# Layer 3's up-projection past the skew as two-by-two blocks in seven products

## The chip, the core and the metric

The kernel runs on one core of a Trainium2 chip. A core has five engines with a queue of instructions each: TensorE (matmuls, PE in the profile, its weight loads PEld), VectorE (DVE), ScalarE (ACT), GpSimd (POOL) and SyncE (SP, which only issues DMAs here). They work out of one on-chip memory (SBUF) and leave matmul results in eight banks of another (PSUM). The metric is device time of one execution in microseconds; the median of the runs shown is 2803.71 us.

## What is computed

The reference is one step of a backbone of four layers on 640 tokens of 1024 features: 512 tokens of a sample and 128 of a prompt, which share all weights. Every layer has a token mixer and then a gated ConvFFN, each between two LayerNorms. The part that matters here is the ConvFFN:

```python
def _conv_ffn(h, w_up, conv_w, conv_b, w_down):
    a, b = jnp.split(h @ w_up, 2, axis=-1)          # h: tokens x 1024, w_up: 1024 x 5632
    ap = jnp.pad(a, ((0, 0), (1, 1), (0, 0)))
    a = ap[:, :-2] * conv_w[0] + ap[:, 1:-1] * conv_w[1] + ap[:, 2:] * conv_w[2] + conv_b
    return (jax.nn.gelu(a) * b) @ w_down            # 2816 -> 1024
```

All is float32. The convolution reads the neighbouring tokens of a, in the sample and in the prompt separately.

## The kernel before, in words

Activations lie feature-major: a ktile is 128 features on the partitions by 640 tokens. Exactness comes from splitting each float32 operand into two parts of a shorter format, hi and lo, that add up to it (`unit` for weights, L157, `split` for activations, L167): ScalarE casts hi (L163, L169), VectorE subtracts it from the original for lo (L164, L170). A product is three matmuls, hi hi, hi lo and lo hi (`mm3`, L175 to L177). The 640 tokens are worked on in two halves, A of 256 and B of 384 columns.

The ConvFFN of a layer has 22 ktiles of 128 hidden features. Ktile j needs two units of weights of w_up, 2j for a and 2j + 1 for b, each [128, 8, 128] (512 KB); the input h is eight ktiles `hs`, hi and lo. Half A of ktiles 0 to 5 runs early, while half B of h is still being made (`ffn_pre`, L529); `skew` (L568) adds their half B, ktile 5 first, 0 last. Ktiles 6 to 21 follow in `up` (L581): for each of the two units the eight-ktile product of half A, then of half B, so 4 x 8 x 3 = 96 matmuls, half with 256 and half with 384 columns. `ffn_a` (L497) copies a out of PSUM on ScalarE into a padded row buffer `ap`. `ffn_g` (L505) then does the convolution (one ScalarE pass and two VectorE passes per segment, L512 and L514), the gelu (L516), the products with b, which is still in PSUM (L518, L519), and the split of the result into an `act` tile (L169, L170).

The down-projection runs in three chunks of ktiles, (0, 7), (7, 14) and (14, 22) (`FFN_CHUNKS`, L40); each chunk's products over its ktiles are added into x for eight output ktiles by VectorE (`evac`, L436). A chunk's down-projection is written behind the first ktile of the next chunk. The last chunk goes through `project` (L440), whose half A's LayerNorm lies beside half B's matmuls. In layers 0 to 2 the FFN also carries the next layer's modulation on VectorE; layer 3 has none.

Tiles come from pools with a fixed number of slots: `actp` 16 (activations in two parts), `hlp` 6 (weights in two parts, 8 KB per partition), `rawp` 4 (weights as loaded), `tmpp` 5, and in PSUM `mmp` 4, `bcp` 3, `stp` 1 banks. The program is not run in the order in which it is written: a scheduler takes, for each engine, the ready instruction that stands earliest in the text, by its own model of times, gives out slots as they come free in that model, and puts in the waits. The order is fixed before the run; on the chip each engine's queue is first in, first out.

Of the kernel before, what the change touches and what calls it, by code (L numbers as in the profile page):

```python
# [33 lines left out]
# half 0 runs ahead of half 1, and 2 of 3 (in front of the pooling, which reads neighbours)  # L34
HALVES = ((0, 256), (256, 640), (0, 384), (384, 640))
HW = 384
# (start, stop, group) with group 0 = sample, 1 = prompt
SEGS = (((0, 256, 0),), ((256, 512, 0), (512, 640, 1)), ((0, 384, 0),), ((384, 512, 0), (512, 640, 1)))
# ktiles of the FFN between its down-projections
FFN_CHUNKS = ((0, 7), (7, 14), (14, 22))  # L40
SKEW = {None: 7, 2: 6, 3: 6, 1: 6, 0: 6}
# units of a projection's weights that half B finds from half A
KEEP = {None: 4, (0, 0): 3, (1, 1): 5, (3, 1): 5, (1, 0): 3, (3, 0): 5}
# layer 0's modulation, blocks of 512 features, in plain float32
MOD32 = (2, 0)
# SKEW ktiles of the FFN run half A ahead of half B, 2 SKEW units of weights: the last SPLIT of them in split parts
# (SPLIT_AHEAD units ahead of their use), of which half B finds the last KEPT; h is split SPLIT_H units from the end
# [29 lines left out]
# columns of the packed per-partition vectors  # L77
# [33 lines left out]
class Kern:  # L111
    def __init__(self, ctx, tc, a):
# [4 lines left out]
        self.actp = P("actp", 16)  # L117
        self.hlp = P("hlp", 6)
# [38 lines left out]
    def unit(self, src, shape, e=None):  # L157
        """A piece of weights, split exactly into two float32r parts."""
        nc = self.nc
        r = self.raw(shape)  # L160
        self.load(r, src)
        hl = self.hlp.tile([128, 2] + list(shape[1:]), F32R, tag="hl", name=self.nm("hl"))
        nc.scalar.copy(hl[:, 0], r)  # L163
        (e or nc.vector).tensor_sub(hl[:, 1], r, hl[:, 0])  # L164
        return hl

    def split(self, dst, src, e=None):  # L167
        """dst [:, 0] + [:, 1] = src exactly."""
# [13 lines left out]
    def table(self, f, x):  # L182
        """Has the tables of an activation function loaded ahead of its use, once x is there."""
        self.nc.scalar.activation(self.small("tab", [128, 1]), x.bitcast(F32), f)

    def consts(self):
# [24 lines left out]
        self.cbc = cp.tile([128, 2, D], F32, name="cbc")  # L211
        self.aps = [cp.tile([128, T + 3], F32, name=f"ap{i}") for i in range(2)]
        self.bgq, self.bgf = [], 0.0
        # modulation [part, chunk, ktile, group]
        self.mod = [cp.tile([128, 6, NK, 2], F32, name=f"mod{i}") for i in range(DEPTH)]

    def cond_rows(self):
        """silu(cond) along the free dimension, on every partition."""
        nc = self.nc
        for g in range(2):  # L220
# [8 lines left out]
    def mod_post(self, L, ft, n, ps, lo=None):  # L229
        """Feature tiles ft .. ft + n (of one chunk) of the modulation of layer L, from its sums [128, n, 2]."""  # L230
# [42 lines left out]
    def mod_dve(self, L, f0, f1):  # L273
        """Feature tiles f0 .. f1 as dot products on the vector engine. Yields after each product."""
# [15 lines left out]
    def bg(self, n):  # L290
        """n steps (on average) of the background work."""
# [18 lines left out]
    def sums_new(self, half):  # L310
        """Sums of z and z^2 over the ktiles, per partition, of a half."""
# [64 lines left out]
    def centre(self, MU, half, ahead):  # L376
        """The ktiles of x of a half less their mean, some ahead of their use."""
# [10 lines left out]
    def ln1(self, t, R, L, which, half, k, S=None):  # L388
        """x <- LN(z) g + b on a ktile of a half."""
# [10 lines left out]
    def ln2(self, t, R, L, ch, half, k, box):  # L400
        """h = LN(x)(1 + scale) + shift on a ktile of a half."""
# [158 lines left out]
    def ffn(self, L, box, side, after):  # L560
# [55 lines left out]
        if L == 0:  # L616
            self.bgq.append(self.mod_dve(0, 40, 48))
# [782 lines left out]
```

## Time and profile before

| what | value |
|---|---|
| median of three runs | 2803.71 us (2803.0 to 2804.68) |
| profiled execution, first to last instruction | 2805.7 us, 2.0 above the median of the runs |
| TensorE busy | 2749.6 us, 98% |
| VectorE busy | 1973.0 us, 70% |
| ScalarE busy | 1240.0 us, 44% |
| GpSimd busy | 407.5 us, 15% |
| the DMA queue of SP | 341.74 MB, 38.7% of 16 engines' time |
| mean granted clock of TensorE | 0.987 |

The profile is of one execution. Durations of TensorE overlap, since matmuls are pipelined: the distance from start to start is what one costs in a row. Durations of VectorE and ScalarE overlap a little too, for the same reason. Layer 3's skew lies at 2362 to 2410 us, its `up` ktiles and down-projections behind that to the end.

### The profile page before, as it was taken

What the parts mean: (1) busy time and instruction counts of PE and PEld (TensorE: products, weight loads), DVE (VectorE), ACT (ScalarE), POOL (GpSimd) and SP (SyncE); (2) the same over time, 40 slices, a digit from 0 to 9 for tenths busy, and PEclk for the clock granted to TensorE, in tenths of its full rate; (3) what the DMA queues carried; (4) which work ended last, traced back from release to release, by engine and by line L of the source; (5) the groups of instructions that cost most, each with busy time, mean ns of one, the idle gap of its engine ahead of it and who ended that gap; (6) DMA issues with size and microseconds to landing.
All of it is one profiled execution on the core that took longest, in us unless ns stands there. A gap on an engine that the chain in (4) does not pass through costs nothing.

```text
span 2805.7 us, 46039 instructions
## 1 busy us (share of the span) xinstructions
PE 2749.6 (98%) x17826; PEld 2636.0 (94%) x17826; DVE 1973.0 (70%) x4263; ACT 1240.0 (44%) x2286; POOL 407.5 (15%) x417
## 2 busy tenths in 40 slices
PE   7999999999999999999999999999999999999998
PEld 4799999999989999999978999999799999999998
DVE  6879977857697887777587878775756558534344
ACT  5656232336496752323367423234532248423233
POOL 1250000024303300000442000005100042000003
PEclk9999999999999999999989999999999999999999
DMA  7735644432402445455104554542422224322221
GB/s 241 259 109 163 198 154 149 156 121 80 134 22 83 136 153 158 149 157 153 56 35 150 151 165 151 158 136 80 161 65 91 68 62 152 97 82 68 83 75 54
DMA packets 99932, 344.70 MB, mean 123 GB/s; under 512 B 11392, under 2 KB 14080, under 8 KB 99584
## 3 DMA queue, kind: packets, MB, share of 16 engines
q1 hardware_dynamic: 99712, 341.74, 38.7%
q8 instruction: 141, 2.31, 0.3%
q14 instruction: 79, 0.65, 0.1%
HBM read 336.19 MB, written 2.88 MB: 121 GB/s over the span
## 4 chain that ended last, share of the span: by engine, by line
PE 88%; DVE 5%; issue 2%; ACT 2%; DMA 2%; POOL 1%; POOLq 0%; ACTq 0%; SPq 0%; DVEq 0%
PE mm L175 26%; PE mm L176 26%; PE mm L177 26%; PE mm L487 2%; PE st L352 1%; PE mm L1157 1%; DVE hl L164 1%; DVE tmp L339 1%; DMA raw<-in_wmod 1%; PE mm L1247 1%; PE bc L372 1%; DVE lnt L383 1%; DVE act L170 0%; PE mm L1072 0%; DMA raw<-in_wup 0%
## 5 line engine op out<-in xcount | busy, mean ns | idle before, releaser
L177 PE MATMUL mm<-act,hl 128*128 128x384 f32 (+2 forms) x4928 | 1528.5, 310 | 3.2 <-DVE hl L164 3.2
L175 PE MATMUL mm<-act,hl 128*128 128x384 f32 (+2 forms) x4928 | 1531.5, 311 | 0.0
L176 PE MATMUL mm<-act,hl 128*128 128x384 f32 (+2 forms) x4928 | 1528.6, 310 | 1.2 <-POOL act L418 1.2
L177 PEld LDWEIGHTS mm<-act,hl 128*128 128x128 f32 x4928 | 935.1, 190 | 5.0 <-DVE hl L164 4.4
L176 PEld LDWEIGHTS mm<-act,hl 128*128 128x128 f32 x4928 | 935.9, 190 | 3.7 <-POOL act L418 1.8
L175 PEld LDWEIGHTS mm<-act,hl 128*128 128x128 f32 x4928 | 935.2, 190 | 3.2 <-ACT hl L163 0.6
L163 ACT CAST hl<-raw 128x1024 fp32r<-128x1024 f32 (+1 forms) x433 | 444.1, 1030 | 625.9 <-PE mm L177 560.1
L164 DVE TENSOR_TENSOR hl<-raw,hl 128x1024 fp32r<-128x1024 f32 (+1 forms) x428 | 526.0, 1231 | 67.4 <-ACT hl L163 65.1
L283 DVE SCALAR_TENSOR_TENSOR bc<-raw,cbc 128x512 f32<-128x512 f32 x608 | 406.2, 719 | 130.3 <-DMA raw<-in_wmod 130.0
L436 DVE SCALAR_TENSOR_TENSOR x<-mm,mod,x 128x256 f32<-128x256 f32 (+2 forms) x408 | 166.0, 434 | 200.4 <-PE mm L177 199.8
L514 DVE SCALAR_TENSOR_TENSOR tmp<-ap,vecs,tmp 128x512 f32<-128x512 f32 x352 | 170.5, 547 | 147.6 <-ACT tmp L512 147.4
L333 POOL TENSOR_TENSOR tmp<-x,tmp 128x256 f32<-128x256 f32 (+1 forms) x180 | 178.0, 993 | 153.2 <-DVE x L436 109.0
L527 POOL MEMSET ap<- 128x1 f32 x24 | 2.1, 99 | 1188.4 <-DVE tmp L514 735.3
L502 ACT COPY ap<-mm 128x256 f32<-128x256 f32 x88 | 33.0, 375 | 265.2 <-PE mm L177 265.2
L333 POOL TENSOR_TENSOR tmp<-x 128x256 f32<-128x256 f32 (+1 forms) x30 | 30.7, 1024 | 733.3 <-DVE x L436 694.5
L383 DVE TENSOR_TENSOR lnt<-x,bc 128x256 f32<-128x256 f32 (+1 forms) x240 | 109.6, 479 | 14.9 <-PE bc L372 14.4
L332 ACT ACTIVATE lnt<-x 128x256 f32<-128x256 f32 (+1 forms) x112 | 51.2, 467 | 133.3 <-DVE x L436 130.9
L516 ACT ACTIVATE tmp<-tmp 128x640 f32<-128x640 f32 x88 | 65.2, 740 | 100.4 <-DVE tmp L514 100.4
L169 ACT CAST act<-tmp 128x640 fp32r<-128x640 f32 x117 | 84.9, 726 | 52.1 <-DVE tmp L519 31.8
L512 ACT ACTIVATE tmp<-ap,vecs 128x512 f32<-128x512 f32 (+1 forms) x176 | 106.4, 658 | 0.0
L339 DVE TENSOR_TENSOR tmp<-tmp,lnt 128x384 f32<-128x384 f32 (+1 forms) x126 | 93.7, 745 | 14.1 <-ACT lnt L332 12.6
L487 PE MATMUL mm<-h,raw 128*128 128x256 f32 x416 | 101.2, 399 | 1.8 <-DVE lnt L404 1.8
(209 smaller groups left out, 2684.1 us busy)
## 6 DMA issues: line engine op xcount, KB each, us to landing
raw<-in_wup SPq DMA_DIRECT2D x216, 512.0 KB, 3.5
raw<-in_wmod SPq DMA_DIRECT2D x184, 512.0 KB, 3.5
raw<-in_wdn SPq DMA_DIRECT2D x64, 448.0 KB, 3.4
raw<-in_wdn SPq DMA_DIRECT2D x46, 512.0 KB, 3.6
raw<-in_wgv SPq DMA_DIRECT2D x24, 512.0 KB, 4.1
raw<-in_wgo SPq DMA_DIRECT2D x19, 512.0 KB, 3.9
raw<-in_wqk SPq DMA_DIRECT2D x18, 512.0 KB, 3.5
raw<-in_wgu SPq DMA_DIRECT2D x16, 512.0 KB, 3.5
```

Of the source, the lines that this page charges most:

```text
L163: nc.scalar.copy(hl[:, 0], r)
L164: (e or nc.vector).tensor_sub(hl[:, 1], r, hl[:, 0])
L175: t.matmul(out, lhs[0], rhs[0], start=start, stop=False)
L176: t.matmul(out, lhs[0], rhs[1], start=False, stop=False)
L177: t.matmul(out, lhs[1], rhs[0], start=False, stop=stop)
L283: nc.vector.scalar_tensor_tensor(out=self.bc(), in0=r[:, sl], scalar=1.0, in1=self.cbc[:, g, sl], op0=ALU.mult, op1=ALU.mult, accum_out=ac ...
L333: nc.gpsimd.tensor_add(S.s[0], z, S.s[0] if n > 1 else S.first)
L339: (self.nc.gpsimd if S.pool else self.nc.vector).tensor_add(S.s[1], S.s[1], S.last)
L383: self.nc.vector.tensor_sub(t, self.x[:, k, a:b], MU)
L436: nc.vector.scalar_tensor_tensor(out=self.x[:, m, s0:s1], in0=ps[:, s0 - a:s1 - a], scalar=sc, in1=self.x[:, m, s0:s1], op0=ALU.mult, op1= ...
L487: self.nc.tensor.matmul(ps, w[:, k, :], h32[:, k, :], start=k == 0, stop=k == NK - 1)
L514: nc.vector.scalar_tensor_tensor(out=c[:, sl], in0=ap[:, o + i:o + i + n], scalar=cw(i), in1=c[:, sl], op0=ALU.mult, op1=ALU.add)
```

## The change

In layer 3, ktiles 6 to 21 of the up-projection (`up7` in place of `up`) are computed as a product of two-by-two blocks with seven block products in place of eight (Winograd's form). The blocks are: of the weights, a1 and a2 (upper and lower 512 of the 1024 input features of unit 2j) and b1, b2 (of unit 2j + 1); of the activations, features 0 to 511 and 512 to 1023, tokens 0 to 319 and 320 to 639. A block product is 4 ktiles x 3 matmuls on 320 columns.

The activations' sums are made once, in `seven_pre`, which the skew steps through behind its last four ktiles: the operands n1, n2, t3 (four ktiles each, hi and lo) go into three new `act` tiles and two `hl` tiles, and t4 at last replaces tokens 320 to 639 of ktiles 0 to 3 of `hs`. The weights' sums are made per ktile on VectorE in a tile S of the `hl` pool. Four tiles of split weights follow: wA (the raw unit 2j), wB and wC (sums) and wD (b2). For wB and wD the lo part is subtracted on VectorE. For wA and wC ScalarE writes the negated cast into the lo part, and a DMA issued by GpSimd adds the original onto it.

Two PSUM banks, X and Z, collect several products one after the other, with their contents copied (ScalarE) or added (VectorE) between two of them; b's part comes out negated, which the multiplication with -1 in `ffn_g` takes back. `ap` is handled as one row of 641 tokens there.

Around it: `FFN_CHUNKS` of layer 3 becomes (0, 6), (6, 11), (11, 15), (15, 22); `actp` has 18 slots, `hlp` 7; the table `cbc` (8 KB per partition, used until layer 2's FFN ends) moves from a place of its own into an `hl` slot; the scratch memory for DMA descriptors is set to 4096. Comments are taken out.

```diff
+SEVEN = (3,)
+HT = T // 2
-FFN_CHUNKS = ((0, 7), (7, 14), (14, 22))
+FFN_CHUNKS = {None: ((0, 7), (7, 14), (14, 22)), 3: ((0, 6), (6, 11), (11, 15), (15, 22))}
-        self.actp = P("actp", 16)
-        self.hlp = P("hlp", 6)
+        self.actp = P("actp", 18)
+        self.hlp = P("hlp", 7)
...
+        if neg:
+            c = self.tmp([128, T + 1])
+            nc.scalar.activation(c, ap[:, 0:T + 1], AF.Identity, scale=cw(0), bias=self.vec(V_CB + L * NJ + j))
+            for i in (1, 2):
+                nc.vector.scalar_tensor_tensor(out=c, in0=ap[:, i:i + T + 1], scalar=cw(i), in1=c, op0=ALU.mult, op1=ALU.add)
+            nc.scalar.activation(c, c, AF.Gelu_apprx_tanh)
+            g = self.tmp([128, T])
+            for x, y, ps in ((0, 0, bA), (HT, HT, bB[:, 0:512 - HT]), (512, 513, bB[:, 512 - HT:HT])):
+                w = ps.shape[1]
+                nc.vector.scalar_tensor_tensor(out=g[:, x:x + w], in0=ps, scalar=-1.0, in1=c[:, y:y + w],
+                                               op0=ALU.mult, op1=ALU.mult)
+            o = self.act()
+            self.split(o, g)
+            return o
...
                 gs[j] = self.ffn_g(L, j, ap, t[:, 1], bB)
+                if j < 4:
+                    steps(pre7, 1)
...
+        def seven_pre():
+            acts = [self.act([128, 2, 2, HT]) for _ in range(3)]
+            hls = [self.hlp.tile([128, 3, 2, HT], F32R, tag="hl", name=self.nm("op")) for _ in range(2)]
+            room = [t[:, i] for t in acts for i in range(2)] + [t[:, i] for t in hls for i in range(3)]
+            n1, n2, t3 = room[0:4], room[4:8], room[8:12]
+            t4 = self.act([128, 4, HT], F32)
+            v = nc.vector
+            fl = lambda x: x.bitcast(F32)
+            for k in range(4):
+                up, lo = fl(hs[k][:, :, :]), fl(hs[k + 4][:, :, :])
+                A, B = slice(0, HT), slice(HT, T)
+                w, z = self.tmp([128, 2, HT]), self.tmp([128, 2, HT])
+                v.tensor_sub(w, up[:, :, A], up[:, :, B])
+                v.tensor_add(w[:, 0], w[:, 0], w[:, 1])
+                self.split(n1[k], w[:, 0])
+                v.tensor_sub(z, lo[:, :, B], up[:, :, B])
+                v.tensor_add(z[:, 0], z[:, 0], z[:, 1])
+                self.split(t3[k], z[:, 0])
+                v.scalar_tensor_tensor(out=z[:, 0], in0=z[:, 0], scalar=-1.0, in1=up[:, 0, A], op0=ALU.mult, op1=ALU.subtract)
+                v.tensor_sub(z[:, 0], z[:, 0], up[:, 1, A])
+                self.split(n2[k], z[:, 0])
+                v.scalar_tensor_tensor(out=z[:, 0], in0=z[:, 0], scalar=-1.0, in1=lo[:, 0, A], op0=ALU.mult, op1=ALU.subtract)
+                v.tensor_sub(t4[:, k], z[:, 0], lo[:, 1, A])
+                yield
+            for k in range(4):
+                self.split(hs[k][:, :, HT:T], t4[:, k])
...
+        def up7(j, ops):
+            v, p = nc.vector, nc.gpsimd
+            ra, rb = self.raw_unit(a["wup"][L, 2 * j]), self.raw_unit(a["wup"][L, 2 * j + 1])
+            new = lambda n=8: self.hlp.tile([128, 2, n, 128], F32R, tag="hl", name=self.nm("hl"))
+            a1, a2, b1, b2 = ra[:, 0:4], ra[:, 4:8], rb[:, 0:4], rb[:, 4:8]
+            S = self.hlp.tile([128, 16, 128], F32, tag="hl", name=self.nm("sums"))
+            v.tensor_add(S[:, 4:8], b1, b2)
+            v.tensor_add(S[:, 0:4], a1, b1)
+            v.tensor_add(S[:, 8:12], a1, S[:, 4:8])
+            v.tensor_add(S[:, 12:16], a2, S[:, 8:12])
+            wA, wB, wC, wD = new(), new(), new(), new(4)
+            def halves(w, x, dma):
+                nc.scalar.copy(w[:, 0], x)
+                if dma:
+                    nc.scalar.activation(w[:, 1], x, AF.Copy, scale=-1.0)
+                    p.dma_start(w[:, 1].bitcast(F32), x, accum_op=ALU.add)
+                else:
+                    v.tensor_sub(w[:, 1], x, w[:, 0])
+            halves(wA, ra, True)
+            halves(wB, S[:, 8:16], False)
+            halves(wC, S[:, 0:8], True)
+            halves(wD, b2, False)
+            X, Y, Z = self.mm([128, HT]), self.mm([128, HT]), self.bc([128, HT])
...
+            ap = self.aps[j % 2]
+            prod(X, wA, 0, ops[0], True)
+            r1 = keep(X)
+            prod(Y, wA, 4, ops[1], True)
+            v.tensor_add(ap[:, 1:1 + HT], r1, Y)
+            prod(X, wB, 0, ops[2], False)
+            r2 = keep(X)
+            prod(Z, wC, 4, ops[3], True)
+            m5 = keep(Z)
+            prod(X, wC, 0, ops[4], False)
+            v.tensor_add(m5, m5, X)
+            prod(Z, wB, 4, ops[5], False)
+            v.tensor_add(ap[:, 1 + HT:513], r2[:, 0:512 - HT], Z[:, 0:512 - HT])
+            v.tensor_add(ap[:, 514:642], r2[:, 512 - HT:HT], Z[:, 512 - HT:HT])
+            prod(X, wD, 0, ops[6], False)
+            gs[j] = self.ffn_g(L, j, ap, X, m5, neg=True)
...
+        self.cbc = self.hlp.tile([128, 2, D], F32, tag="hl", name="cbc")
...
+    nc = _bacc.Bacc("TRN2", target_bir_lowering=False, num_devices=1,
+                    dynamic_dma_scratch_size=4096)
```

Here `prod(ps, w, k0, rhs, first)` is the four-ktile product with `mm3`, `keep` copies a bank into SBUF on ScalarE, and ops[0] to ops[6] are, in this order: features 0 to 511 and 512 to 1023 of tokens 0 to 319, n2, n1, t3, features 512 to 1023 of tokens 320 to 639, and t4.

## Rows read from the trace of the kernel before

**Rows 1.** The page: span, busy time (share, instructions), shares of the chain.
```profile
span 2805.7 us, 46039 instructions
PE 2749.6 (98%) x17826; PEld 2636.0 (94%) x17826; DVE 1973.0 (70%) x4263; ACT 1240.0 (44%) x2286; POOL 407.5 (15%) x417
PE 88%; DVE 5%; issue 2%; ACT 2%; DMA 2%; POOL 1%; POOLq 0%; ACTq 0%; SPq 0%; DVEq 0%
```
**Rows 2.** Windows: stretch, length, busy of PE PEld DVE ACT POOL, PEclk, DMA, GB/s.
```profile
2400.00:2450.00 50.00, 50.00 (x334) 50.00 (x333) 25.05 (x41) 19.54 (x31) 0.00 (x0) 1.00 0.30 87
2450.00:2500.00 50.00, 50.00 (x344) 50.00 (x344) 19.95 (x33) 10.92 (x14) 0.00 (x0) 1.00 0.25 75
```
**Rows 3.** Timeline of TensorE: start, us, engine, line, operation, tiles, shape.
```profile
2399.67 0.33 PE L175 MATMUL mm<-act,hl 128*128 128x384 f32 x1
...
2410.42 0.33 PE L177 MATMUL mm<-act,hl 128*128 128x384 f32 x1
2410.59 0.28 PE L175 MATMUL mm<-act,hl 128*128 128x256 f32 x1
...
2411.90 0.28 PE L177 MATMUL mm<-act,hl 128*128 128x256 f32 x1
...
2424.66 0.28 PE L175 MATMUL mm<-act,hl 128*128 128x256 f32 x1
```
**Rows 4.** Timeline of VectorE, in brackets the idle time before and its end.
```profile
2359.84 0.56 DVE L418 TENSOR_TENSOR act<-lnt,act 128x384 fp32r<-128x384 f32 x1 [0.20 <-ACT act L417]
...
2383.35 1.94 DVE L514 SCALAR_TENSOR_TENSOR tmp<-ap,vecs,tmp 128x512 f32<-128x512 f32 x4
2385.20 1.22 DVE L164 TENSOR_TENSOR hl<-raw,hl 128x1024 fp32r<-128x1024 f32 x1
2386.34 0.42 DVE L518 TENSOR_TENSOR tmp<-tmp,act 128x256 f32<-128x256 f32 x1
2386.67 0.55 DVE L519 TENSOR_TENSOR tmp<-tmp,mm 128x384 f32<-128x384 f32 x1
```
**Rows 5.** Timeline of ScalarE in the skew.
```profile
2371.00 1.21 ACT L512 ACTIVATE tmp<-ap,vecs 128x512 f32<-128x512 f32 x2
2372.10 2.00 ACT L163 CAST hl<-raw 128x1024 fp32r<-128x1024 f32 x2
2373.99 0.75 ACT L516 ACTIVATE tmp<-tmp 128x640 f32<-128x640 f32 x1
...
2382.06 0.36 ACT L502 COPY ap<-mm 128x256 f32<-128x256 f32 x1
2382.33 0.27 ACT L503 COPY ap<-mm 128x128 f32<-128x128 f32 x1
```
**Rows 6.** DMA issues of 2400 to 2800: count, KB each, median us to landing.
```profile
raw<-in_wup SPq DMA_DIRECT2D x28, 512.0 KB, 3.4
...
out_y<-x SPq DMA_DIRECT2D x8, 192.0 KB, 1.9
out_y<-x SPq DMA_DIRECT2D x2, 128.0 KB, 1.7
```
**Rows 7.** Groups of 2300 to 2806: count | busy, mean ns | idle before.
```profile
L164 DVE TENSOR_TENSOR hl<-raw,hl 128x1024 fp32r<-128x1024 f32 x65 | 82.3, 1268 | 14.2 <-ACT hl L163 14.0
...
L360 POOL TENSOR_TENSOR lnv<-lnw,mhalf 128x2 f32<-128x2 f32 x2 | 1.4, 703 | 2.7 <-DVE lnw L359 2.6
```
**Rows 8.** Windows of the skew and the start of `up`.
```profile
2368.90:2371.90 3.00, 3.00 (x19) 2.93 (x18) 0.05 (x2) 1.33 (x4) 0.96 (x1) 1.00 0.61 175
2389.00:2414.10 25.10, 25.10 (x154) 25.10 (x153) 17.33 (x28) 15.75 (x26) 0.00 (x0) 1.00 0.43 120
```
**Rows 9.** Windows around a wait of TensorE.
```profile
2345.00:2347.40 2.40, 0.69 (x6) 0.49 (x5) 2.40 (x3) 2.40 (x7) 1.98 (x3) 1.00 0.00 0
2347.40:2351.60 4.20, 4.18 (x24) 4.18 (x24) 4.20 (x5) 2.89 (x5) 0.85 (x1) 0.63 0.49 152
```
**Rows 10.** Timelines: VectorE and GpSimd side by side, before the skew.
```profile
2345.35 2.02 DVE L164 TENSOR_TENSOR hl<-raw,hl 128x1024 fp32r<-128x1024 f32 x1
...
2346.46 1.79 POOL L333 TENSOR_TENSOR tmp<-x,tmp 128x384 f32<-128x384 f32 x1 [0.17 <-ACT x L396]
```

More of the change, by code (lines that the diff above doesn't have):

```diff
@@ L170, in split, with mm3 @@
         (e or self.nc.vector).tensor_sub(dst[:, 1], src, dst[:, 0])
-    def mm3(self, out, lhs, rhs, start, stop):
+    def mm3(self, out, lhs, rhs, start, stop, on=False):
         t = self.nc.tensor
-        t.matmul(out, lhs[0], rhs[0], start=start, stop=False)
-        t.matmul(out, lhs[0], rhs[1], start=False, stop=False)
-        t.matmul(out, lhs[1], rhs[0], start=False, stop=stop)
+        t.matmul(out, lhs[0], rhs[0], start=start, stop=False, skip_group_check=on)
+        t.matmul(out, lhs[0], rhs[1], start=False, stop=False, skip_group_check=on)
+        t.matmul(out, lhs[1], rhs[0], start=False, stop=stop, skip_group_check=on)
     def vec(self, col, n=1):
@@ L210, in consts @@
         nc.vector.tensor_sub(self.condr[:, :, 2:4], self.cond, self.condr[:, :, 0:2])
-        self.cbc = cp.tile([128, 2, D], F32, name="cbc")
         self.aps = [cp.tile([128, T + 3], F32, name=f"ap{i}") for i in range(2)]
@@ L503, in ffn_a, with ffn_g @@
             nc.scalar.copy(ap[:, 514:642], ps[:, 256:384])
-    def ffn_g(self, L, j, ap, bA, bB):
+    def ffn_g(self, L, j, ap, bA, bB, neg=False):
         nc = self.nc
         cw = lambda i: self.vec(V_CW + (3 * L + i) * NJ + j)
+        if neg:
[12 more added lines that the diff above has]
+            return o
         c = self.tmp([128, T])
@@ L566, in wu, with skew @@
             return self.unit(a["wup"][L, i], [128, NK, 128])
-        def skew():
+        def skew(pre7):
             for j in range(at(SKEW, L) - 1, -1, -1):
@@ L614, in down @@
                     self.bg(at(BG, L))
+        def seven_pre():
[24 more added lines that the diff above has]
+                self.split(hs[k][:, :, HT:T], t4[:, k])
+            b = lambda k, sl: (hs[k][:, 0, sl], hs[k][:, 1, sl])
+            pair = lambda t: (t[:, 0], t[:, 1])
+            yield ([b(k, slice(0, HT)) for k in range(4)], [b(k + 4, slice(0, HT)) for k in range(4)],
+                   [pair(t) for t in n2], [pair(t) for t in n1], [pair(t) for t in t3],
+                   [b(k + 4, slice(HT, T)) for k in range(4)], [b(k, slice(HT, T)) for k in range(4)])
@@ new lines, in up7, with prod, keep @@
+        def up7(j, ops):
[21 more added lines that the diff above has]
+            X, Y, Z = self.mm([128, HT]), self.mm([128, HT]), self.bc([128, HT])
+            def prod(ps, w, k0, rhs, first):
+                for k in range(4):
+                    self.mm3(ps, (w[:, 0, k0 + k], w[:, 1, k0 + k]), rhs[k], first and k == 0, k == 3, not first)
+            def keep(ps):
+                t = self.small("lnt", [128, HT], LNT)
+                nc.scalar.copy(t, ps)
+                return t
+            ap = self.aps[j % 2]
[3 more added lines that the diff above has]
+            v.tensor_add(ap[:, 1:1 + HT], r1, Y)
+            self.bg(at(BG, L))
+            prod(X, wB, 0, ops[2], False)
+            r2 = keep(X)
+            prod(Z, wC, 4, ops[3], True)
+            m5 = keep(Z)
+            self.bg(at(BG, L))
+            prod(X, wC, 0, ops[4], False)
[3 more added lines that the diff above has]
+            v.tensor_add(ap[:, 514:642], r2[:, 512 - HT:HT], Z[:, 512 - HT:HT])
+            self.bg(at(BG, L))
+            prod(X, wD, 0, ops[6], False)
+            self.bg(at(BG, L))
+            gs[j] = self.ffn_g(L, j, ap, X, m5, neg=True)
@@ L616, in ffn @@
         if L == 0:
             self.bgq.append(self.mod_dve(0, 40, 48))
+        ops = None
         pend = None
-        for ci, (k0, k1) in enumerate(FFN_CHUNKS):
+        for ci, (k0, k1) in enumerate(at(FFN_CHUNKS, L)):
             if ci == 0:
-                skew()
+                pre7 = seven_pre() if L in SEVEN else iter(())
+                skew(pre7)
+                ops = next(pre7, None)
             for j in range(max(k0, at(SKEW, L)), k1):
-                up(j)
+                if ops is not None:
+                    up7(j, ops)
+                else:
+                    up(j)
@@ L1385 @@
     ins = _layout({k: np.asarray(v) for k, v in inputs.items()})
-    nc = _bacc.Bacc("TRN2", target_bir_lowering=False, num_devices=1)
+    nc = _bacc.Bacc("TRN2", target_bir_lowering=False, num_devices=1,
+                    dynamic_dma_scratch_size=4096)
     aps, arrays = {}, {}
```

## The prediction

> **What bounds the kernel now.** I read the page first: busy shares and the chain of waits [rows 1]. TensorE is busy for 2749.6 of 2805.7 us and holds 88% of the chain, so what counts is matmul time and whatever makes TensorE wait. Then the windows of layer 3's FFN [rows 2]: TensorE is busy for all 50 us of each window, VectorE for 20 to 25, ScalarE for 11 to 20, GpSimd for none. TensorE sets the pace there and the others have room. Third, the timeline of TensorE [rows 3] gives the price of a matmul: 63 matmuls of 384 columns start between 2399.67 and 2410.42 us, one every 173.4 ns; 12 of 256 columns start between 2410.59 and 2411.90, one every 119.1 ns. The slope is 54.3 ns for 128 columns, so 320 columns, which the trace does not show, cost halfway: 146.2 ns. One ktile of the up-projection (`up(j)`) takes 48 of each, 14.04 us; the trace has 14.07 (2410.59 to 2424.66).
>
> **Removed on TensorE.** Per ktile, 96 matmuls become seven products of 4 ktiles times 3 matmuls, 84 of 320 columns: 12.28 us, 1.76 less. There are 16 ktiles (6 to 21): -28.1 us. The down-projection keeps its 1056 matmuls; its fourth chunk adds 8 evacuations of 256 and 16 of 128 columns, some 9 us by the rule below for VectorE, which is idle for 25 to 30 of 50 us there [rows 2]: nothing.
>
> **Is another engine the bound then?** Back to back, a VectorE operation costs less than its own duration: 1.14 us for 1024 elements, 0.33 for 256, and 1.85 for the four of the convolution [rows 4]; so about n/0.96 ns + 0.07 us, and 0.13 us with a scalar. Per ktile now: four sums of 512 (2.4), remainders of 1024 and 512 (1.7), four additions from PSUM (1.3), convolution over 641 columns (1.6), three products (1.05), the split (0.75): 8.8 us of 12.28. ScalarE: a cast of 1024 is 0.95 us [rows 5], five of these (two of them the negated copies) 4.75, one of 512 (0.53), three copies of 320 from PSUM (1.0), and convolution (0.82, by the 1.10 of its two parts), gelu and split (0.75 each) 2.3: 8.6 of 12.28. Both stay near 70%: hidden as long as nothing waits on them at once. It does at three places: between two uses of the bank X (or Z) lies one product, 1.75 us, in which ScalarE must copy the bank, or VectorE add it. The copy (0.36) or addition (0.40) fits even behind one operation of 0.95 or 1.14 us, not behind two. I charge 0.1 us per ktile: +1.5 us (bounds 0 and 10).
>
> **Added: the loop through the weight slots.** The operand tiles hold two of the seven `hl` slots for the whole stretch, which leaves five, just S, wA, wB, wC and wD of one ktile. A tile of the next ktile starts when one of this ktile is let go. The tight one is wC: the third to be needed (fourth product) and given the slot of wB, which product 6 reads last. From there: two ScalarE passes over 1024 (1.95 us), issue on GpSimd, the adding DMA's landing (call it D), then products 4, 5 and 6 (36 matmuls, 5.26 us) until the slot is free again. With three hand-overs (VectorE starts 0.20 us behind ScalarE [rows 4]; I take 0.2 to 0.25 each) and 0.3 us of waiting for ScalarE, together 1.0 us, the loop is 8.2 us + D. wA has the same loop through S, since S is held until the DMA of wC has read it. GpSimd's queue holds nothing else here [rows 2]; SP's two loads per ktile stay, and its four `raw` slots cover two ktiles though the first is held until its DMA lands. Behind a late landing stand all later matmuls of the ktile and, where S waits for its slot, VectorE's sums.
>
> The trace has no adding DMA and none issued by GpSimd. Below, D is a plain load of the same 512 KB, 3.4 us; above, two of these in a row, 6.8 [rows 6]. The nearest rows have an SBUF source: 1.7 us for 128 KB and 1.9 for 192 KB, 0.2 per 64 KB over 1.3 fixed, so 512 KB move in 1.6. An addition reads source and destination, twice 1.6 over 1.3: 4.5, and 5.2 if GpSimd spends 0.7 us on the issue, as on its smallest arithmetic [rows 7]. I take 4.8. The loop is 13.0 us against 12.28, 0.72 late. It binds in 12 of 16 ktiles: 6, 7, 12 and 16 find their tiles made, in the skew or during a down-projection. +8.6 us.
>
> **Added: preparing the operands.** `seven_pre` adds on VectorE, per k of four, two operations of 640 (0.74), four additions and three remainders of 320 (0.40) and two with a scalar (0.46): 5.2 us, 20.0 in all up to the last n2, which the third product of ktile 6 reads. With the sums and wB's remainder (3.5) it is due by 2414.1 on the old clock (2410.6, the end of the skew, plus two products). In 2389.0 to 2414.1 VectorE works 17.33 of 25.1 us [rows 8]; 2.3 of that (units of the old `up(6)`) goes and 2.0 (down units) can be later, so 36.5 us of work stand against 25.1: 11.4 short. Of these 2.9 fit into the hole at 2368.9 [rows 8], since a scheduler lets ready work pass. +8.5 us, in the skew or at the third product. After such a gap TensorE restarts slowly: behind the wait at 2345 (0.69 of 2.40 us busy), 24 matmuls of 256 columns took 4.20 us at a granted clock of 0.63 (the chip alternates there between 1.2 and 2.4 GHz), where 35 fit at full clock: 11 x 0.119, +1.4 us [rows 9]. Bounds of both together: 3 and 18.
>
> **The rest.** `cbc` takes the seventh `hl` slot until layer 2 ends, so layers 0 to 2 keep six. Two more `act` slots and a rescheduled order may move waits there: within 3 us either way, I take 0.
>
> **Sum.** -28.1 + 1.5 + 8.6 + 8.5 + 1.4 = -8.1 us on the profiled 2805.7, so 2797.6. The median of the runs, 2803.7, lies 2.0 below that execution: 2796.
>
> **Rivals.** (1) The adding DMA lands late, and it gets slower. The place is the loop: each microsecond of D over 4.1 costs 12. The other terms leave 16.7 us of gain, so the sign turns at D = 5.5. At the upper bound, 6.8, it costs 32.6: 2820. For it: nothing in the trace shows the unit's rate. Against: a store shows 1.3 us that don't grow with size, so D need not double.
> (2) GpSimd's issue is held up by VectorE. The trace shows the two engines in each other's way: beside a GpSimd addition the remainder of 1024 took 2.02 us against 1.27 on average [rows 7, 10]. If each issue waits for one such operation (1.14), D is 5.9, the loop 14.1, 22.3 us lost: 2809, slower at the edge of what can be told. Against: an issue has no tile to read. The Trainium skill, page SBUF — State Buffer, section "SBUF: two separate sides", holds that DMAs issued from GpSimd are special in this: their descriptors can't be written while a VectorE operation in a two-port mode has the port that the two engines share. By that rule the time would be this rival's 2809 or less, as only such operations block; the two rows agree that the engines block each other, and no row shows it for an issue.
> (3) The DMA lands within 4.1 us: the loop is covered and -16.7 stays: 2787. For it: if source and destination are read side by side, D is 1.3 + 1.6 = 2.9 and an issue [rows 6]. Against: an addition moves three streams where a copy moves two.
> (4) Preparation costs its upper bound, 18 instead of 9.9, because its chain of split and subtract goes back and forth between VectorE and ScalarE and the hole at 2368.9 stays empty: 2804, no change. For it: such hand-overs; against: other work of VectorE can stand between them.
>
> **How the numbers follow.** Forecast 0.40, rival 1 0.13, 2 0.11, 3 0.21, 4 0.15. What this kernel's measurement can tell from no change is 0.2%, 5.6 us: 2798.1 to 2809.3. The forecast itself runs from 2787 to 2806 (D from 4.1 to 5.2, the other bounds partly): 0.28 faster, 0.11 no change, 0.01 slower. With 3 wholly faster, 4 mostly no change (0.12; 0.02 faster, 0.01 slower), 2 half no change (0.05) and half slower, 1 slower: faster 0.51, same 0.28, slower 0.21. The range 2780 to 2816 leaves out the far half of rival 1 and the best of rival 3.
>
> **What would show it.** Right: 84 matmuls of 320 columns per ktile at 146 ns; ktiles 8 to 11, 13 to 15 and 17 to 21 at about 13 us with a wait of 0.7 before product 4 (or product 1), put down to an `hl` tile or its DMA; one TensorE gap of 6 to 10 us near the third product of ktile 6 or spread over the last three of the skew. Wrong: a 320-column matmul far from 146 ns; ktiles at 12.3 (rival 3) or over 13.8 us (1 and 2); no gap at ktile 6; VectorE or ScalarE above 90% there; or a shift of more than 3 us before 2340.

## The result, and the profile after

The changed kernel takes 2822.8 us (median of 4 runs, 2819.4 to 2828.0) against 2803.7 before: ratio 1.0069, 95% interval 1.0054 to 1.0083, so 0.7% slower. I had forecast 2796, faster, with a range up to 2816. The profiled execution has a span of 2826.0 us, 20.3 more than [rows 1]. In every run that has both on record, the time of an execution lies 1.7 to 2.3 us above its span. So the profiled execution of before is one of some 2807.6 us, 4 above its median, and the profiled one of after, 2828.0, is 5 above its median. Its page:

```profile
span 2826.0 us, 46081 instructions
PE 2734.8 (97%) x17634; PEld 2611.7 (92%) x17634; DVE 2053.9 (73%) x4455; ACT 1302.5 (46%) x2358; POOL 433.3 (15%) x449
```

TensorE is busy for 15 us less and the span is 20 longer: some 35 us more in which it does nothing. Where it lies is read from the windows of layer 3's FFN, in which [rows 2] had 50 of 50 us and a granted clock of 1.00 (columns as there):

```profile
2400.00:2450.00 50.00, 41.48 (x217) 39.20 (x218) 43.08 (x78) 27.53 (x50) 1.93 (x2) 0.88 0.38 104
2450.00:2500.00 50.00, 50.00 (x340) 50.00 (x339) 26.82 (x51) 15.54 (x19) 1.73 (x2) 1.00 0.40 108
2500.00:2550.00 50.00, 46.74 (x312) 45.39 (x310) 29.44 (x53) 31.13 (x44) 6.62 (x8) 1.00 0.59 136
```

The first stretch (skew and ktile 6) loses 8.5 us and part of the clock; the second, a down-projection, nothing; the third, ktiles in seven products, 3.3. The waits of TensorE in the ktiles from 7 on (2494 to 2761) and, in the second block, in the skew (2380 to 2437), each with total, number and longest:

```profile
PE mm L178 <- ACT lnt L706: 8.6, 9, 1.1
PE bc L180 <- DMA hl<-sums: 3.2, 6, 1.6
PE mm L180 <- DMA hl<-raw: 0.4, 1, 0.4
```

```profile
PE mm L178 <- ACT hl L166: 11.0, 2, 5.6
```

The forecast had the second line. It did not have the first (copies of the products' banks on ScalarE) nor the last (the cast of a plain weight unit in the skew).

From the first matmuls of the LayerNorm (LN) sums ahead of this FFN (2351.4 us before, 2360.7 after), of ktiles 7 to 21 and of the last LN, the difference divides as follows. A ktile without a wait took 12.31 us and a ktile of the down-projection 7.03, so up to ktile 7 an undisturbed run needs 59.2 (old skew) + 12.3 + 6 x 7.03 = 113.7 us; it took 133.65. Ktiles 7 to 21 need 184.7 and took 203.05.

| term | forecast | measured |
|---|---|---|
| matmuls of 16 ktiles | -28.1 | -27.7 |
| skew and ktile 6, with the half clock | +9.9 | +20.0 |
| ktiles 7 to 21 | +10.1 | +18.3 |
| layers 0 to 2 | 0 | +9.3 |
| rest | 0 | +0.4 |
| sum | -8.1 | +20.3 |

**The skew.** ScalarE's timeline there:

```profile
2398.39 0.46 ACT L172 CAST act<-tmp 128x320 fp32r<-128x320 f32 x1 [1.88 <-DVE tmp L653]
2398.80 0.46 ACT L172 CAST op<-tmp 128x320 fp32r<-128x320 f32 x1
2399.16 1.99 ACT L166 CAST hl<-raw 128x1024 fp32r<-128x1024 f32 x2
```

and TensorE's:

```profile
2394.52 0.34 PE L180 MATMUL mm<-act,hl 128*128 128x384 f32 x1
2400.25 0.69 PE L178 MATMUL mm<-act,hl 128*128 128x384 f32 x1 [5.39 <-ACT hl L166]
```

The two casts that TensorE needs stand directly behind the first write of an operand tile (`op`, a slot of the same `hl` pool), and that write waits for VectorE's preparation (L653). The same picture comes again 16 us later, behind the first write of the second operand tile.

**A ktile.** ScalarE at the boundary of ktiles 8 and 9:

```profile
2510.28 0.74 ACT L518 ACTIVATE tmp<-tmp 128x641 f32<-128x641 f32 x1 [1.18 <-DVE tmp L517]
2512.19 1.05 ACT L688 CAST hl<-raw 128x1024 fp32r<-128x1024 f32 x1 [1.17 <-DMA hl<-sums]
2513.15 1.05 ACT L690 ACTIVATE hl<-raw 128x1024 fp32r<-128x1024 f32 x1
2514.10 0.71 ACT L172 CAST act<-tmp 128x640 fp32r<-128x640 f32 x1
2514.71 0.41 ACT L706 COPY lnt<-mm 128x320 f32<-128x320 f32 x1
```

and TensorE there:

```profile
2511.80 0.31 PE L180 MATMUL mm<-op,hl 128*128 128x320 f32 x1
...
2515.18 0.41 PE L178 MATMUL mm<-op,hl 128*128 128x320 f32 x1 [1.13 <-ACT lnt L706]
```

The cast at 2512.19 is the next ktile's wA. It waits until wC's adding DMA has landed, and its negated copy and a split follow. The copy of bank X, whose last matmul starts at 2511.80, stands behind all three: 2514.71. The fifth product, the next in bank X, starts at 2515.18.

**Layers 0 to 2.** ScalarE at the end of the Fourier layer, before and then after:

```profile
89.77 1.05 ACT L163 CAST hl<-raw 128x1024 fp32r<-128x1024 f32 x1 [0.77 <-DMA raw<-in_wmod]
...
92.51 1.91 ACT L226 COPY cbc<-mm 128x512 f32<-128x512 f32 x3 [0.36 <-PE mm L224]
```

```profile
97.00 0.73 ACT L172 CAST act<-tmp 128x640 fp32r<-128x640 f32 x1
97.63 2.05 ACT L230 COPY cbc<-mm 128x512 f32<-128x512 f32 x4
99.53 0.77 ACT L172 CAST act<-tmp 128x640 fp32r<-128x640 f32 x1
100.16 3.92 ACT L166 CAST hl<-raw 128x1024 fp32r<-128x1024 f32 x4
```

Four casts of weights now lie behind the first write of `cbc`, which now is an `hl` tile; in the kernel before such casts run ahead of it. TensorE waits 2.4 us for them and then has a granted clock of 0.66 in 100 to 110 us, 1.00 in the kernel before:

```profile
101.30 0.58 PE L178 MATMUL mm<-act,hl 128*128 128x256 f32 x1 [2.38 <-ACT hl L166]
```

There is a loss ahead of this, at 50 to 60 us: TensorE is busy for 6.41 us at a clock of 0.66, before for 9.22 at 1.00. At the first LN sums of the program, which start at 139.1 us before and at 147.9 after, 8.8 of the 9.3 us are there.

**The theories.** A: a tile that takes a slot of a shared pool and is first written late holds back the casts of the units that stand behind it in the text, as if slots were handed out in the order of the text (`cbc`, `op`). B: VectorE's backlog from the preparation, as forecast. C: wC's DMA holds S, S's slot holds wA's cast, that cast holds ScalarE's copies. D: VectorE or ScalarE simply has too much to do per ktile.

### The profile page after: what moved, and what is told of

Same layout as the page of the kernel before. It is cut to its first block, busy times and chain, and to the rows that moved or that the text cites. A ratio compares the mean times of both kernels' runs of the same rounds, so it can differ in the third digit from the quotient of the medians.

```text
span 2826.0 us, 46081 instructions
## 1 busy us (share of the span) xinstructions
PE 2734.8 (97%) x17634; PEld 2611.7 (92%) x17634; DVE 2053.9 (73%) x4455; ACT 1302.5 (46%) x2358; POOL 433.3 (15%) x449
## 5 line engine op out<-in xcount | busy, mean ns | idle before, releaser
L178 PE MATMUL mm<-act,hl 128*128 128x384 f32 (+3 forms) x4640 | 1445.8, 312 | 13.6 <-ACT hl L166 13.4
L180 PE MATMUL mm<-act,hl 128*128 128x384 f32 (+3 forms) x4640 | 1441.0, 311 | 4.0 <-DVE hl L167 3.5
L179 PE MATMUL mm<-act,hl 128*128 128x384 f32 (+3 forms) x4640 | 1442.2, 311 | 2.7 <-POOL act L422 1.8
L178 PEld LDWEIGHTS mm<-act,hl 128*128 128x128 f32 x4640 | 882.2, 190 | 18.2 <-ACT hl L166 15.1
L179 PEld LDWEIGHTS mm<-act,hl 128*128 128x128 f32 x4640 | 882.9, 190 | 5.2 <-POOL act L422 2.5
L180 PEld LDWEIGHTS mm<-act,hl 128*128 128x128 f32 x4640 | 881.7, 190 | 5.7 <-DVE hl L167 4.7
L166 ACT CAST hl<-raw 128x1024 fp32r<-128x1024 f32 (+4 forms) x409 | 411.4, 1012 | 516.4 <-PE mm L180 433.0
L167 DVE TENSOR_TENSOR hl<-raw,hl 128x1024 fp32r<-128x1024 f32 (+4 forms) x404 | 486.0, 1206 | 57.4 <-ACT hl L166 54.3
L440 DVE SCALAR_TENSOR_TENSOR x<-mm,mod,x 128x256 f32<-128x256 f32 (+2 forms) x432 | 175.6, 434 | 186.3 <-PE mm L180 185.6
L533 DVE SCALAR_TENSOR_TENSOR tmp<-ap,vecs,tmp 128x512 f32<-128x512 f32 (+1 forms) x288 | 139.7, 545 | 57.3 <-ACT tmp L531 57.2
L172 ACT CAST act<-tmp 128x640 fp32r<-128x640 f32 (+1 forms) x123 | 87.6, 712 | 67.0 <-DVE tmp L538 34.9
L173 DVE TENSOR_TENSOR act<-tmp,act 128x640 fp32r<-128x640 f32 (+1 forms) x123 | 98.7, 802 | 20.3 <-ACT act L172 19.5
L535 ACT ACTIVATE tmp<-tmp 128x640 f32<-128x640 f32 x72 | 53.3, 740 | 98.0 <-DVE tmp L533 97.9
L400 ACT ACTIVATE x<-lnt,vecs 128x256 f32<-128x256 f32 (+1 forms) x128 | 82.2, 647 | 27.9 <-DVE lnt L399 27.2
```

Source lines behind the costliest of these rows:

```text
L173: (e or self.nc.vector).tensor_sub(dst[:, 1], src, dst[:, 0])
L178: t.matmul(out, lhs[0], rhs[0], start=start, stop=False, skip_group_check=on)
L179: t.matmul(out, lhs[0], rhs[1], start=False, stop=False, skip_group_check=on)
L180: t.matmul(out, lhs[1], rhs[0], start=False, stop=stop, skip_group_check=on)
L440: nc.vector.scalar_tensor_tensor(out=self.x[:, m, s0:s1], in0=ps[:, s0 - a:s1 - a], scalar=sc, in1=self.x[:, m, s0:s1], op0=ALU.mult, op1= ...
L533: nc.vector.scalar_tensor_tensor(out=c[:, sl], in0=ap[:, o + i:o + i + n], scalar=cw(i), in1=c[:, sl], op0=ALU.mult, op1=ALU.add)
```

## The experiments

Each was timed beside the kernel before, on three occasions: e1 to e4 (before: 2805.0 us), e5 to e8 (2805.0) and e9 to e12 (2807.1); the changed kernel was first timed beside 2803.7. So differences between medians of two occasions carry some 1 to 3 us; the ratios, each to the kernel before beside it, don't. The columns in the middle are worked out from each profile as in the table above: us later than before at the LN ahead of layer 3's FFN, us lost from there through ktile 6 (through the plain ktiles where there are some), and us lost in the other ktiles.

| run | median us | ratio, 95% | layers 0-2 | skew, ktile 6 | ktiles |
|---|---|---|---|---|---|
| changed kernel | 2822.8 | 1.0054 to 1.0083 | 9.3 | 20.0 | 18.3 |
| the same again (e12) | 2822.7 | 1.0043 to 1.0067 | 2.9 | 20.8 | 18.5 |
| e1 storage alone | 2812.8 | 1.0015 to 1.0035 | 4.4 | - | - |
| e2 cbc early | 2816.2 | 1.0023 to 1.0047 | 0.2 | 19.2 | - |
| e3 operands early | 2818.4 | 1.0034 to 1.0060 | 4.1 | 17.1 | - |
| e4 exchanged | 2808.1 | 1.0002 to 1.0020 | 2.9 | 22.0 | 1.3 |
| e5 late preparation | 2805.0 | 0.9991 to 1.0009 | 6.4 | 0.3 | 17.4 |
| e6 copy on VectorE | 2815.9 | 1.0029 to 1.0056 | 3.0 | 21.2 | 16.2 |
| e7 no DMA | 2807.5 | 1.0002 to 1.0019 | 2.6 | 24.1 | 0.1 |
| e8 three edits | 2782.7 | 0.9910 to 0.9935 | -3.1 | 1.3 | 1.0 |
| e9 half preparation | 2810.2 | 1.0000 to 1.0018 | 5.8 | 8.0 | - |
| e10 one plain ktile | 2786.3 | 0.9918 to 0.9944 | -3.2 | 6.5 | 0.5 |
| e11 e8 without DMA | 2783.2 | 0.9900 to 0.9928 | 0.7 | 0.9 | 0.0 |

**e1, storage alone** (the kernel before with these lines):

```diff
-        self.actp = P("actp", 16)
-        self.hlp = P("hlp", 6)
+        self.actp = P("actp", 18)
+        self.hlp = P("hlp", 7)
...
-        self.cbc = cp.tile([128, 2, D], F32, name="cbc")
+        self.cbc = self.hlp.tile([128, 2, D], F32, tag="hl", name="cbc")   # in cond_rows
...
+                    dynamic_dma_scratch_size=4096)
```

> The kernel before with the change's storage alone: cbc as a tile of the hl pool, first written in cond_rows near the end of the Fourier layer, seven hl slots, eighteen act slots, the smaller DMA scratch; no product in seven. Theory A (slots of a pool are handed out in the order of the text, so a tile that is first written late holds back the casts of the weight units that stand behind it in the text): TensorE waits near 50 and 98 us as in the changed kernel, the LN sums of layer 0 stand 9 us later than before, and the whole takes about 2812 us (2803.7 + 9). Rival (the 9 us come from the new code of layer 3, through the scheduler, and not from storage): 2804, and no late events before layer 3. Second rival (more act slots help elsewhere): below 2803.

2812.8, 7.9 over the kernel before: the loss needs nothing of layer 3's new code. The rivals fall. ScalarE has the casts behind `cbc` here too:

```profile
94.80 2.05 ACT L226 COPY cbc<-mm 128x512 f32<-128x512 f32 x4
...
97.33 3.93 ACT L163 CAST hl<-raw 128x1024 fp32r<-128x1024 f32 x4
```

**e2, cbc written early:**

```diff
+        self.cbc = self.hlp.tile([128, 2, D], F32, tag="hl", name="cbc")   # in consts
+        nc.vector.memset(self.cbc[:, 0, 0:2], 0.0)
```

> The changed kernel with cbc allocated in consts and two of its elements written there, so that it has its hl slot from the start; cond_rows only fills it. Theory A: the casts of layer 0 go back to their old places, everything before layer 3 comes 9 us earlier, about 2814 us (2822.8 - 9). Rival (layer 0 loses its 9 us because one slot fewer is left for the units, or to the changed load order): no change, 2823.

2816.2, 6.6 less than the changed kernel. ScalarE's timeline now has the casts ahead of `cbc`, one of them alone behind its last part:

```profile
84.91 1.08 ACT L166 CAST hl<-raw 128x1024 fp32r<-128x1024 f32 x1
...
87.04 1.05 ACT L166 CAST hl<-raw 128x1024 fp32r<-128x1024 f32 x1
89.15 1.05 ACT L166 CAST hl<-raw 128x1024 fp32r<-128x1024 f32 x1 [1.06 <-PE mm L180]
...
91.89 1.91 ACT L231 COPY cbc<-mm 128x512 f32<-128x512 f32 x3
```

The nine profiles with a late `cbc` stand 2.6 to 9.3 us later than before at layer 3, 4.6 on average; the four with an early one -3.2 to 0.7. Nearer to the cause, at the first LN sums (139.1 us before), the two kinds stand clearly apart: the nine are 4.9 to 8.8 us later, 6.9 on average, the four -0.4 to 1.9. The loss at 50 to 60 us goes too: TensorE is busy there for 9.21 us at 1.00 again. The number of slots and buffers is the same, so it is the late place of `cbc` in the text, its allocation with its first write: theory A. (This edit moves both; e3 moves a first write alone.)

**e3, operand tiles written early** (in `seven_pre`, behind their allocation):

```diff
+            for t in hls:
+                nc.scalar.copy(t[:, 0, 0, 0:2], self.identr[:, 0:2])
```

> The changed kernel with two elements of each of the two operand tiles in the hl pool written as soon as they are allocated in seven_pre. Theory A: the casts of the last six weight units of the skew no longer queue on ScalarE behind the first split into these tiles; the two waits of TensorE in the skew (5.73 and 5.94 us) and the half clock behind them go, and 10 to 14 us with them: about 2811. Ktile 6 may give some of it back, since the operands themselves are made no earlier. Rival B (what I forecast: VectorE has 11 us more work than time before the third product of ktile 6): the waits move to ktile 6 and the time stays within 3 us of 2823.

2818.4, 4.4 less; the ratios of the two (1.0034 to 1.0060, and 1.0043 to 1.0083 in the two timings of the changed kernel) overlap, so the profile has to tell. The skew itself is as short as before (59.7 us from the LN sums to its end, 59.2 before), so A is right for the two waits in it. But most of the time comes back at ktile 6. Its waits, and windows of the stretch:

```profile
PE mm L178 <- ACT hl L690: 8.8, 1, 8.8
PE mm L180 <- DMA hl<-raw: 1.9, 1, 1.9
PE bc L180 <- DMA hl<-sums: 1.2, 1, 1.2
```

```profile
2395.00:2405.00 10.00, 10.00 (x60) 10.00 (x59) 10.00 (x21) 6.62 (x15) 0.00 (x0) 1.00 0.21 70
2405.00:2415.00 10.00, 10.00 (x60) 10.00 (x59) 10.00 (x21) 6.59 (x14) 1.05 (x1) 1.00 0.04 8
...
2425.00:2435.00 10.00, 3.62 (x12) 3.22 (x13) 9.31 (x19) 5.87 (x9) 0.88 (x1) 0.54 0.15 43
```

VectorE (third engine column) is busy for all 20 us from 2395 to 2415 and TensorE then stands for 8.8 us before ktile 6's third product, at a granted clock of 0.54 in 2425 to 2435: B, where I had put it. Of the 10 to 14 us that A promised 4.4 are left; the two causes stand one behind the other, and taking away the first alone uncovers the second.

**e4, the exchange:**

```diff
-            halves(wC, S[:, 0:8], True)
-            halves(wD, b2, False)
+            halves(wC, S[:, 0:8], False)
+            halves(wD, b2, True)
```

> The changed kernel with the remainder of wC (1024 per partition) on VectorE and that of wD (512) by the adding DMA, so that half as many bytes per ktile plus wA's go by DMA and the sums tile S is never read by one. Theory C (the ktiles lose their time to wC's DMA: the fourth product waits 0.3 to 1.0 us for it, and the fifth 1.2 to 1.45 us because S's slot stays taken until that DMA lands, the next wA's cast waits for the slot, and ScalarE's copy of bank X stands behind that cast): both waits go, the ktiles 8 to 11, 13 to 15 and 17 to 21 go from 12.9 to 15.3 us to 12.3 to 12.6, some 15 us in all, about 2808. Rival D (VectorE or ScalarE cannot keep up in a ktile of 12.3 us, whatever the slots): VectorE gets 0.6 us more to do per ktile, the ktiles stay at 13.5 us or more, 2820 or above.

2808.1, 14.7 less, with more work for VectorE: D falls, C holds. Every ktile takes 12.31 or 12.32 us but one, and of all the waits of the ktiles (2490 to 2740) one is left:

```profile
PE mm L180 <- DMA hl<-raw: 1.0, 1, 1.0
```

**e5, the preparation in plain ktiles 6 and 7** (and the operand tiles written early as in e3):

```diff
-                skew(pre7)
-                ops = next(pre7, None)
+                skew(iter(()))
...
+                if j < at(SKEW, L) + 2:
+                    steps(pre7, 2)
+                elif ops is None:
+                    ops = next(pre7, None)
```

> The changed kernel with the operands made later: the skew is left alone as in the kernel before, ktiles 6 and 7 go as plain products with two steps of the preparation each, the operand tiles' first elements are written at once, and the seven products begin with ktile 8. Two ktiles more cost 14.05 instead of 12.3 us. Theory E (the 17 to 20 us lost between the skew's start and the end of ktile 6 come from making the operands there, in ScalarE's queue and on VectorE; VectorE is idle half the time in plain ktiles, where the same work is hidden): the skew takes 40 us again, no wait over 2 us at ktile 6 to 8, and about 2806 us (2822.8 - 20 + 3.5). Rival (the work has no room in plain ktiles either, since ScalarE's casts stand behind its hand-overs with VectorE there too): a wait of 5 us or more at ktile 8, 2815 or above.

2805.0, 17.7 less, as expected: 0.3 us are lost through ktile 7, where the changed kernel loses 20.0 through ktile 6.

**e6, the second copy of X on VectorE:**

```diff
-            r2 = keep(X)
+            r2 = self.small("lnt", [128, HT], LNT)
+            v.tensor_copy(r2, X)
```

> The changed kernel with the second copy of bank X (r2) on VectorE instead of ScalarE, so that it does not stand behind the next wA's cast. Theory C (this copy is late because ScalarE is held by a cast that waits for S's slot): the 1.2 to 1.45 us that the fifth product waits go; the loop through wC's slot and its DMA stays, with 13.0 us by my forecast's working against ktiles of 14.0 now: some 8 us less, about 2814. Rival (the fifth product waits because ScalarE has too much to do, or the fourth's wait merely grows by the same amount): ktiles stay at 13.8 or more, 2821 to 2824.

2815.9. The fifth product's wait goes, as C says, but the ktiles lose 16.2 us where they lost 18.3: the fourth product now waits up to 2.7 us for wC's DMA. The rival was right about the size. The DMA rows of 2500 to 2700 show why:

```profile
hl<-sums POOLq DMA_DIRECT2D x11, 512.0 KB, 5.8
hl<-raw POOLq DMA_DIRECT2D x10, 512.0 KB, 4.5
```

wC's DMA lands after 5.8 us instead of 4.8. So with copies out of the way the loop of the forecast is there, and D is no constant. (Of the 6.9 us in the median only these 2 lie in the ktiles. The profiled execution, 2821.3, was the slowest of five, and executions of one program differ by as much: 2817.3 to 2828.0 for the changed kernel.)

**e7, no adding DMA** (`True` replaced by `False` for wA and wC).

> The changed kernel with all remainders on VectorE and no adding DMA. VectorE gets 2 x 1.14 us more per ktile (wA and wC, 1024 each), 11.1 of 12.3 by my working, and ScalarE two passes of 0.95 less. Theory C (only what hangs on the landing of wC's DMA slows the ktiles): ktiles at 12.3 to 12.6 and about 2808, like the run with the DMAs exchanged. Rival D (VectorE is needed for the additions from PSUM just when it makes remainders, 90% busy): ktiles of 13 us or more, 2817 or above; then the adding DMAs do earn something.

2807.5, and no ktile from 7 on above 12.32 us. VectorE is busy for 40.96 of 49 us in ktiles 7 to 10, 84%, without a wait: the adding DMAs earn nothing here.

**e8, three edits** (those of e2, e4 and e5).

> Three edits together: cbc written early, wC's and wD's remainders exchanged, operands made in plain ktiles 6 and 7. If the three causes stand beside each other, the gains measured alone and expected add up: 2822.8 - 6.6 (measured) - 14.8 (measured, of which nothing is at ktile 6) - 16 (expected of the late operands) = 2785, faster than the kernel before by 19. By the matmuls alone: 14 ktiles x 1.75 = 24.5 less than before, 2779. If the late operands fall through: about 2801.

2782.7 us, ratio to the kernel before 0.9922 (0.9910 to 0.9935): faster by 22. The gains measured alone, 6.6 + 14.7 + 17.7 = 39.0, leave 2783.8 of 2822.8: the three causes stand beside each other, within the 1 to 3 us between occasions. The page, and windows of skew, plain ktiles and down-projection:

```profile
span 2781.7 us, 46107 instructions
PE 2721.5 (98%) x17658; PEld 2606.0 (94%) x17658; DVE 2052.4 (74%) x4442; ACT 1292.6 (46%) x2354; POOL 425.9 (15%) x445
```

```profile
2374.00:2404.00 30.00, 30.00 (x175) 30.00 (x174) 23.19 (x38) 19.49 (x36) 0.00 (x0) 1.00 0.38 109
2404.00:2432.00 28.00, 28.00 (x190) 28.00 (x189) 25.97 (x51) 13.36 (x25) 0.00 (x0) 1.00 0.28 80
2432.00:2480.00 48.00, 48.00 (x328) 48.00 (x327) 28.97 (x58) 15.39 (x26) 1.93 (x2) 1.00 0.24 74
```

In the plain ktiles VectorE takes the preparation at 93% while TensorE never stops.

**e9, half the preparation** (e3, with operands made for k = 0 and 1 only and used twice).

> The run with the operand tiles written early (2818.4 us), which waits 9.1 us for the second product of ktile 6 and some 17 us in all at that ktile, with half the preparation left out: operands are made for k = 0 and 1 alone and used again for 2 and 3, the second half of hs keeps its old contents there; the products and their weights stay. Theory B (once ScalarE's casts are free, VectorE's 20 us of preparation are the limit, 11 us more than there is time): with 10 us less the loss at ktile 6 falls from 17 to 5 us or less, about 2805. Rival (the loss is the chain of hand-overs between VectorE and ScalarE, or the wait of the next weights for a slot, which stays half or whole): 2810 or above.

The loss falls from 17.1 to 8.0 us, 2810.2: it halves with the work, but does not go, and by the bounds set beforehand this is the rival's side. (In e3 the long wait is at the third product of ktile 6, not at the second, as I wrote above: 24 matmuls of two products lie ahead of it.) Of the 8.0, 4.7 are a wait for wA's adding DMA, which GpSimd issues at 2417.38, behind ScalarE's negated copy. VectorE's load is about half, hand-overs and ScalarE's queue can be the rest; how the rest divides stays open.

**e10, one plain ktile instead of two** (e8 with all four steps in ktile 6).

> The fastest version (2782.7 us: cbc early, remainders exchanged, two plain ktiles with the preparation) with the whole preparation in one plain ktile, 6, and seven products from ktile 7: 1.75 us less of matmuls. Theory B: a plain ktile leaves VectorE about 8 us free and the preparation needs 20, so TensorE waits some 9 us at ktile 7: 2790. Rival (the scheduler spreads it, the room of one ktile and the first products of the next is enough): 2781.

2786.3, 3.7 more than e8 though one ktile has 1.75 us less to do; the ratios overlap, but the loss through the plain ktiles rises from 1.3 to 6.5 us. TensorE waits for VectorE's evacuations once:

```profile
2427.80 0.34 PE L180 MATMUL mm<-act,hl 128*128 128x384 f32 x1
2431.52 0.39 PE L178 MATMUL mm<-act,hl 128*128 128x256 f32 x1 [3.38 <-DVE x L441]
```

I had expected 9 us of waiting and got 3.4, at the first bank that VectorE has to clear rather than at ktile 7: B in kind, less in size.

**e11, e8 without DMAs** (`False` for all four).

> The fastest version with all remainders on VectorE instead of the exchange. If adding DMAs earn nothing at 12.3 us per ktile (VectorE stays under 90%), 2781 to 2785, the same; if VectorE is short while the first operands and the down-projection's units are made beside the ktiles, waits at ktile 8 or behind the down-projections and 2787 or above.

2783.2: the same as e8.

**e12, the changed kernel again.**

> The changed kernel as it is, on the chip of the last three, since its profiled execution was the slowest of four (2828.0 of 2819.4 to 2828.0). What layer 0 loses before layer 3 was 2 to 6 us in the profiles of the other runs with its start, not 9: here about 5, the skew and ktile 6 about 20, the ktiles from 7 on 7 to 9 less than in the kernel before, 2818 to 2823 in all. If layer 0 loses 9 again, the late cast costs more than the runs with an early cbc gave back.

2822.7 once more, with 2.9 us instead of 9.3 lost before layer 3. Skew and ktiles repeat to within a microsecond. Of the 6.4 us between the two executions, 2.8 lie ahead of the first LN sums (6.0 us late here, 8.8 there) and 3.6 between there and layer 3. On that second stretch the thirteen profiles lie between 0.5 us behind and 4.7 ahead of the one profile of before; the cause stays open, and part may be that profile's own, of an execution 4 us above its median.

## Why the prediction was wrong

**Right.** A 320-column matmul starts every 146 ns; an undisturbed ktile takes 12.31 us for 12.28; the matmuls give 27.7 for 28.1. The adding DMA lands 4.8 us after its issue begins, as taken:

```profile
hl<-raw POOLq DMA_DIRECT2D x16, 512.0 KB, 4.5
hl<-sums POOLq DMA_DIRECT2D x16, 512.0 KB, 4.8
```

so rival 1 (D = 6.8) and rival 3 (4.1) fell. From wC's cast (2505.10) to the next (2519.00) the loop takes 13.90, of which 1.3 is the wait for the copy: 12.6 without it, for the 13.0 forecast. The next round takes 14.11 (to 2533.11), so the sign set for rivals 1 and 2, ktiles over 13.8 us, appeared without either.

**Rival 2 fell.** GpSimd's 32 issues take 0.86 to 1.05 us and begin 0.3 to 0.6 behind ScalarE's copy. They do so also beside VectorE, here in the exchanged version, first GpSimd's row, then VectorE's:

```profile
2613.18 0.87 POOL L691 DMA_DIRECT2D hl<-raw  x1 [7.17 <-ACT hl L690]
```

```profile
2612.85 0.69 DVE L680 TENSOR_TENSOR sums<-raw 128x512 f32<-128x512 f32 x1
2613.45 0.88 DVE L517 SCALAR_TENSOR_TENSOR tmp<-ap,vecs,tmp 128x641 f32<-128x641 f32 x1
```

The Trainium skill, page SBUF — State Buffer, section "SBUF: two separate sides", says that VectorE keeps GpSimd from writing descriptors while it runs in its two-port modes. No issue here shows such a hold-up; the operations beside these issues have two input tensors. Whether a plain float32 copy within SBUF would cause one was not tried.

**Wrong, step by step.** (1) "I charge 0.1 us per ktile" for bank X: the fifth product starts 1.0 to 1.3 us late in eight ktiles and 0.5 in a ninth. I wrote that wA has the same loop through S, and that the copy fits behind one ScalarE operation but not behind two, and did not put the two together: a cast that waits for S's slot stands still at the head of an in-order queue, and the bank copies of TensorE are behind it. Of the idle time in the ktiles 8.6 us are the copy's, where 1.5 was charged, and 3.6 the adding DMAs', where the loop was charged 8.6; with the slower starts around these waits it is 18.3 for 10.1. The copy is not a price by itself: without its wait (e6) the landing takes its place, and only without a DMA that reads S (e4) both go. (2) Preparation: 20.0 for 9.9, rival 4's upper bound of 18 was nearer. The backlog of VectorE was the right mechanism, but only in part (e3, e9), and its price too small; ahead of it stood the casts behind the operand tiles' first writes, which I did not see, since I treated two `hl` slots as merely taken. (3) "Within 3 us" for layers 0 to 2: 4.6 on average and 9.3 in the profiled execution, by the same mechanism with `cbc`, so the last sign of being wrong, a shift of more than 3 us before 2340, came true; I had counted its slots and not asked when it is first written. Each of the three alone would have left a time of 2804 to 2806, within the range; together, with 0.4 of the rest, they are 28 us over the terms charged, 2796 + 28 = 2824. No rival gave this time for its reason: rival 1 has 2820 at its upper bound, by a landing of 6.8 us that did not come.

## What to carry to other kernels

Ask of a tile that moves into a shared pool when it is first written, not only how many slots it takes: giving `cbc` its place early, by a write of two elements, gave some 6 us here. Where an instruction waits for a slot, price everything behind it on its engine, above all copies that free PSUM; a DMA that merely reads a tile prolongs that tile's life by its whole landing time. Put one-time preparation where its engine has room: two plain ktiles cost 3.5 us and saved 20.

## What the runs showed of the hardware that was not expected

The landing time of an adding DMA of 512 KB is not fixed: 4.5 to 4.8 us in the changed kernel, 5.8 in e6, where one took 6.1 with a weight load in flight; but in the changed kernel one took 4.7 beside a load (2507 to 2513), so what lengthens it stays open. One of 256 KB took 3.3 (e8, median). Two waits in the skew, 5.7 and 5.9 us from start to start, cost more than their length. Behind the first one the granted clock was 0.50 from 2400 to 2404 us, its lower level of 1.2 GHz: the first matmuls of 384 columns started up to 0.49 us apart and the next ones every 0.32, until 2404.9, where they had started every 0.17. That is 2.4 us more for these 13.
